# Down projection by seven block products, with weight block sums on GpSimd and the residual stream kept token-major

## The chip, the cores and the metric

One core of a Trainium2 chip runs the program. The metric is device time in microseconds (us). Engines: PE (TensorE, matrix products), DVE (VectorE) and ACT (ScalarE) for elementwise work, POOL (GpSimd) for elementwise work in SBUF, SP (SyncE), which issues the weight transfers.

## What is computed

Two encoder layers over 256 tokens of width 2048, all in float32: an RMS norm, one input projection, three kinds of attention, an output projection added to the residual stream `x`, and then a gated feed-forward block (FFN) added to `x`, which is the part that changes:

```python
def conv_ffn(x, w_up, conv_w, conv_b, w_down):       # x (256, 2048), w_up (2048, 11264), w_down (5632, 2048)
    h = x @ w_up
    hp = jnp.pad(h, ((0, 0), (1, 1), (0, 0)))
    h = hp[:, :s] * conv_w[0] + hp[:, 1:s + 1] * conv_w[1] + hp[:, 2:] * conv_w[2] + conv_b
    gate, up = jnp.split(h, 2, axis=-1)
    return (jax.nn.silu(gate) * up) @ w_down
...
        x = x + y @ w_out[l]
        x = x + conv_ffn(rms_norm(x, ffn_norm[l]), w_up[l], conv_w[l], conv_b[l], w_down[l])
    return rms_norm(x, final_norm)
```

## The kernel before

**Number format.** Every float32 product is made of three products of rounded operands (fp32r): with `a = ah + al` and `w = wh + wl`, it takes `ah*wh + al*wh + ah*wl`. So each weight chunk that lands in SBUF (tile `wland`, 128 partitions x 1024 values, 512 KB) passes ACT, which rounds it to `wh` (`emit_high`, L291), and DVE, which subtracts `wl = wland - wh` (`emit_low`, L302). Both read SBUF alone. There are 5 landing buffers and 3 to 4 buffers for the two parts (L276). 802 chunks are used in the whole run.

**Layout.** The residual stream is held transposed: `x[m]` has 128 of the 2048 features on partitions and all 256 tokens along the free axis. The activations of a product are pairs of tiles `pg` (high and low part, 256 tokens each).

**FFN.** 44 blocks `f` of 128 columns make up the 5632 hidden features. `up(g)` (L1041) computes the gate half and the up half of 11 such blocks; each block takes four chunks, and each chunk eight matmuls of 512 columns (the stationary `wh` block against high and low activations side by side) and eight of 256 (`wl` against the high ones). `conv_gen` (L1004) follows per block: ACT copies the PSUM result to `hs`, DVE adds the other half, DVE multiplies by the norm factor `rall`, ACT and DVE do the three-tap convolution (`scalar_tensor_tensor`, four per block), ACT the silu, DVE the gate product, and ACT and DVE split the result into high and low part. `down(g)` (L1084) multiplies 11 hidden blocks by `w_down`, for eight pairs of 128 output features, through `cols` (L393). Its first three groups use 512-column matmuls (`joint`), the last one 256-column matmuls. `down_gen` adds the sums to `x`. The four groups run as up(0), up(1), down(0), up(2), down(1), up(3), down(2), down(3).

**Output projection.** The same `cols`, with 256-column matmuls.

**Order.** All engines follow a static order. The PE order is the order of the code; the other steps are generators, which `pump` (L340) advances between matmuls when a small cost model (`Clock`, `Engine.cost`, L145) says that their inputs are there. POOL does only the norm's power function on a few values and the small rope tables (L1101).

Of the kernel before, what the change touches and what calls it, by code (L numbers as in the profile page):

```python
# [33 lines left out]
FGRP = 4  # L35
FPG = NF // FGRP

# [21 lines left out]
def plan():  # L59
# [7 lines left out]
    def down(g):  # L67
        for m in range(KD // 2):
            cols("w_down", list(range(g * FPG, (g + 1) * FPG)), m * 256, 256)

    def up(g):
        for f in range(g * FPG, (g + 1) * FPG):
            for half in range(2):
                for base in (0, DFF):
                    out.append(("w_up", list(range(half * 8, half * 8 + 8)), base + f * P, P))
# [12 lines left out]
    for ks in (Y_BA, Y_C):  # L88
        for m in range(KD // 2):
            cols("w_out", ks, m * 256, 256)  # L90
    up(0)
    for g in range(1, FGRP):
        up(g)
        down(g - 1)
    down(FGRP - 1)
    return out


PLAN = plan()
# [4 lines left out]
for _name, _w in (("attn_norm", 16), ("ffn_norm", 16), ("out_norm", 16), ("c_q_norm", 4), ("c_kv_norm", 4),  # L104
                  ("conv_w0", 88), ("conv_w1", 88), ("conv_w2", 88), ("conv_b", 88), ("final_norm", 16)):
    VEC[_name] = _n
    _n += _w
# [31 lines left out]
class Engine:  # L139
# [5 lines left out]
    def cost(self, op, aps, out):  # L145
        n = out.free_size()
        if self.name == "pe":
            return n * (1 if aps[1].dtype == F32R else 4) / 2.4
        if self.name == "act":
            return (112 + n) / 1.2 + 93 * sum(a.free_size() == 1 for a in aps[1:])  # L150
        return (66 + n) / 0.96 if self.name == "dve" else 500 + n / 0.6
# [36 lines left out]

class Fixed:
# [14 lines left out]
class Norm:  # L204


    def __init__(self, parts, width, squares):
        self.parts, self.left, self.width, self.squares = parts, parts, width, squares
        self.rows, self.all = [], []


class Group(Norm):


    def __init__(self, heads, k0, act, gain, squares):
        super().__init__(heads, heads * HD, squares)
# [4 lines left out]
class Kern:  # L221
    def __init__(self, tc, ctx, a):
# [7 lines left out]
        self.n_dma = self.n_high = self.n_low = self.n_use = 0  # L230
        self.land, self.high, self.parts, self.ready, self.ends = {}, {}, {}, {}, []
        self.chunks = []
        off = {m: 0 for m in MATS}
        for layer in range(DEPTH):
            for mat, ks, c0, w in PLAN:
                sz = len(ks) * w
                self.chunks.append((mat, off[mat], len(ks), w))
                off[mat] += sz * P
# [4 lines left out]
        self.pg = Slots(self.clock, self.sb, 39, "pg", [P, 2, S])  # L243
        self.pp = Slots(self.clock, self.sb, 6, "pp", [P, 2, S])
        self.tm = Slots(self.clock, self.sb, 3, "tm", [P, NB, 512])
        self.scr = Slots(self.clock, self.sb, 2, "scr", [P, NB, 512])
# [31 lines left out]
    def emit_dma(self):  # L278
        i = self.n_dma
        if i < len(self.x):  # L280
            self.load(self.nc.sync, self.x[i], self.a["x"][i].rearrange("p (j s) -> p j s", j=2))
        mat, off, nk, w = self.chunks[i]
        sz = nk * w
        t = self.t("wland", [P, CHUNK], self.LAND)
        c = self.clock
        c.at["dma"] = max(c.at["dma"], c.at["dve"])
        self.load(self.nc.sync, t[:, :sz], self.a[mat][off:off + P * sz].rearrange("(p f) -> p f", p=P))
        self.land[i] = t
        self.n_dma += 1

    def emit_high(self):  # L291
        i = self.n_high
        _, _, nk, w = self.chunks[i]
# [4 lines left out]
        self.ac.copy(h[:, :sz], self.land[i][:, :sz])  # L298
# [3 lines left out]
    def emit_low(self):  # L302
        i = self.n_low
        _, _, nk, w = self.chunks[i]
# [5 lines left out]
        self.ve.tensor_tensor(lo[:, :sz], self.land.pop(i)[:, :sz], h[:, :sz].bitcast(F32), ALU.subtract)  # L310
# [4 lines left out]
    def prefetch(self):  # L315
# [4 lines left out]
        while self.n_dma < min(n, self.LAND):  # L320
            self.emit_dma()
        while self.n_high < min(n, u + ahead + (u > 0)):
            if self.n_high >= self.n_dma:
                self.emit_dma()
# [5 lines left out]
        while self.n_dma < min(n, self.n_low + self.LAND):  # L330
            self.emit_dma()
# [61 lines left out]
    def cols(self, pm, act, ks, free, joint=False):  # L393

        mmul = self.te.matmul
        for run in k_runs(ks, 256):
            wh, wl = self.use()
            for i in range(2):
                cs = slice(i * P, (i + 1) * P)
                o = pm[:, i, :S]  # L400
                for j, k in enumerate(run):
                    self.drain(lambda: k in act)
                    x, first = act[k], k == ks[0]
                    if joint:
                        mmul(pm[:, i], wh[:, j, cs], x.rearrange("p s n -> p (s n)"), start=first, stop=False)
                    else:
                        mmul(o, wh[:, j, cs], x[:, 0], start=first, stop=False)
                        mmul(o, wh[:, j, cs], x[:, 1], start=False, stop=False)
# [42 lines left out]
    def new_norm(self):  # L451
        return Norm(KD // 2, D, self.t("sqx", [P, S], 2))
# [6 lines left out]
    def x_parts(self, m, act, gain):  # L459

        x = self.x[m]
        yield from self.until(x)
        sl = yield from self.take(self.pg, 2, F32R)
        for i in range(2):
            self.ac.activation(sl[i][:, 0], x[:, i], AF.Copy, scale=gain[:, 2 * m + i:2 * m + i + 1])
        for i in range(2):
            h, lo = self.hl(sl[i])
            self.ve.scalar_tensor_tensor(lo, x[:, i], gain[:, 2 * m + i:2 * m + i + 1], h.bitcast(F32),
                                         ALU.mult, ALU.subtract)
            act[2 * m + i] = sl[i]  # L470
        yield

    def add_squares(self, norm, x):

        yield from self.until(x)
# [788 lines left out]
```

## Time and profile before

| | us |
|---|---|
| median of 3 runs | 2286.79 (2286.78 to 2286.97) |
| profiled execution, its own time | 2286.59 |
| span of the profile, first to last instruction | 2284.8 |
| PE busy | 2263.7 (99%) |
| DVE busy | 1644.1 (72%) |
| ACT busy | 1217.7 (53%) |
| POOL busy | 32.9 (1%) |

The span is cut by stage as follows: the FFN of layer 0 runs from 398.9 to 1140.3 us on PE and that of layer 1 from 1529.5 to 2270.9 us. TensorE's granted clock is 1.00 in both stretches, which is the 2.4 GHz level. The rest is attention, the projections around it, a start of about 6 us and a tail of about 14 us. A busy time is the union of an engine's instruction spans; spans of consecutive instructions overlap a little, so the distance from start to start is what an instruction costs in a full queue.

### The profile page before, as it was taken

What the parts mean: (1) busy time and instruction counts of PE and PEld (TensorE: products, weight loads), DVE (VectorE), ACT (ScalarE), POOL (GpSimd) and SP (SyncE); (2) the same over time, 40 slices, a digit from 0 to 9 for tenths busy, and PEclk for the clock granted to TensorE, in tenths of its full rate; (3) what the DMA queues carried; (4) which work ended last, traced back from release to release, by engine and by line L of the source; (5) the groups of instructions that cost most, each with busy time, mean ns of one, the idle gap of its engine ahead of it and who ended that gap; (6) DMA issues with size and microseconds to landing.
All of it is one profiled execution on the core that took longest, in us unless ns stands there. A gap on an engine that the chain in (4) does not pass through costs nothing. (4 is left out here: it accounts for less than half of the span.)

```text
span 2284.8 us, 34786 instructions
## 1 busy us (share of the span) xinstructions
PE 2263.7 (99%) x13452; PEld 2009.3 (88%) x13452; DVE 1644.1 (72%) x2369; ACT 1217.7 (53%) x1778; POOL 32.9 (1%) x51
## 2 busy tenths in 40 slices
PE   8999999999999999999999999999999999999997
PEld 7889889888888888888988898898888888888897
DVE  6577778777766776776756877787777677667755
ACT  6456745555544554553545566555555455445543
POOL 1000000000000000000010000000000000000000
PEclk9999999999999999999999999999999999999999
DMA  7544435555555555555554444465555555555553
GB/s 275 183 147 149 161 116 189 193 185 191 186 180 198 187 186 190 191 181 186 191 188 173 157 148 140 136 198 185 188 190 184 185 194 191 181 194 191 182 186 121
DMA packets 119110, 410.15 MB, mean 180 GB/s; under 512 B 13344, under 2 KB 13856, under 8 KB 118944
## 3 DMA queue, kind: packets, MB, share of 16 engines
q1 hardware_dynamic: 118800, 407.90, 52.4%
q8 instruction: 105, 1.72, 0.3%
q14 instruction: 61, 0.50, 0.1%
q10 hardware_dynamic: 144, 0.03, 0.0%
HBM read 405.78 MB, written 2.10 MB: 179 GB/s over the span
## 5 line engine op out<-in xcount | busy, mean ns | idle before, releaser
L164 DVE TENSOR_TENSOR wl<-wland,wh 128x1024 fp32r<-128x1024 f32 (+2 forms) x802 | 943.6, 1177 | 497.3 <-PE mm L164 448.0
L164 PE MATMUL mm<-pg,wh 128*128 128x512 f32 (+1 forms) x5472 | 1274.1, 368 | 0.4 <-DVE pg L164 0.4
L164 ACT CAST wh<-wland 128x1024 fp32r<-128x1024 f32 (+2 forms) x802 | 810.7, 1011 | 761.3 <-PE mm L164 399.7
L164 PEld LDWEIGHTS mm<-pg,wh 128*128 128x128 f32 x5472 | 905.6, 190 | 120.0 <-PE mm L164 0.7
L164 PEld LDWEIGHTS mm<-pg,wl 128*128 128x128 f32 x4832 | 690.2, 190 | 60.3
L164 PE MATMUL mm<-pg,wl 128*128 128x256 f32 x4832 | 724.4, 282 | 0.0
L164 PE MATMUL mm<-wh,pg 128*128 128x512 f32 (+3 forms) x1504 | 435.9, 366 | 6.4 <-ACT pg L164 6.4
L164 PEld LDWEIGHTS mm<-wh,pg 128*128 128x128 f32 x1504 | 272.7, 189 | 46.6 <-ACT pg L164 6.4
L164 PE MATMUL mm<-wl,pg 128*128 128x512 f32 (+3 forms) x752 | 272.6, 362 | 0.3 <-DVE wl L164 0.2
L164 DVE SCALAR_TENSOR_TENSOR pp<-hs,vecs,pp 128x256 f32<-128x256 f32 x352 | 162.3, 482 | 6.3
L164 PEld LDWEIGHTS mm<-wl,pg 128*128 128x128 f32 x752 | 142.7, 190 | 19.8 <-DVE wl L164 1.2
L164 DVE TENSOR_TENSOR x<-x,mm 128x512 f32<-128x512 f32 x160 | 109.2, 683 | 6.9 <-PE mm L164 4.7
L164 ACT ACTIVATE pp<-hs,vecs 128x256 f32<-128x256 f32 x176 | 96.2, 594 | 15.5 <-DVE hs L164 15.5
L164 ACT CAST pg<-pp 128x256 fp32r<-128x256 f32 x88 | 35.8, 407 | 89.6 <-DVE pp L164 89.5
L164 ACT ACTIVATE pp<-pp 128x256 f32<-128x256 f32 x88 | 36.9, 419 | 86.7 <-DVE pp L164 86.7
L164 DVE TENSOR_TENSOR pg<-pp,pg 128x256 fp32r<-128x256 f32 x88 | 37.4, 425 | 38.7 <-ACT pg L164 38.7
L164 DVE TENSOR_TENSOR hs<-hs,rall 128x512 f32<-128x512 f32 x88 | 60.9, 692 | 3.1
L164 DVE TENSOR_TENSOR hs<-mm,hs 128x512 f32<-128x512 f32 x88 | 60.1, 683 | 0.0
L164 ACT COPY hs<-mm 128x512 f32<-128x512 f32 x88 | 51.1, 580 | 0.0
L164 PE MATMUL at<-pg,pg 128*128 128x256 f32 (+1 forms) x288 | 43.4, 294 | 0.0
L164 PEld LDWEIGHTS at<-pg,pg 128*128 128x128 f32 x288 | 38.3, 192 | 3.4 <-DVE pg L164 0.4
L164 POOL TENSOR_TENSOR small<-small,cst 128x2 f32<-128x2 f32 (+1 forms) x19 | 19.0, 1004 | 1480.4 <-DVE small L164 1480.4
(87 smaller groups left out, 790.8 us busy)
## 6 DMA issues: line engine op xcount, KB each, us to landing
wland<-in_w_up SPq DMA_DIRECT2D x352, 512.0 KB, 3.5
wland<-in_w_in SPq DMA_DIRECT2D x144, 512.0 KB, 3.5
wland<-in_w_down SPq DMA_DIRECT2D x128, 512.0 KB, 3.6
wland<-in_w_out SPq DMA_DIRECT2D x64, 384.0 KB, 3.0
wland<-in_w_down SPq DMA_DIRECT2D x64, 384.0 KB, 3.1
wland<-in_w_out SPq DMA_DIRECT2D x16, 512.0 KB, 3.5
wland<-in_w_ukv SPq DMA_DIRECT2D x12, 512.0 KB, 3.4
wland<-in_w_in SPq DMA_DIRECT2D x8, 480.0 KB, 3.2
```

The costliest lines, as they stand in the source:

```text
L164: return f(*args, **kw)
```

## The change

1. The down projection is done in 2x2 blocks after Strassen and Winograd, with seven products in place of eight. The hidden blocks come in 11 groups of four (`FPG = 4`). In each group the activation is split by token half (two of 128) and by feature half, and the weight by feature half and by output half (512 columns each, two column pairs `cp` cover 2048). Each product has 256 hidden features (two `j`), the stationary operand is an activation of 128 x 128, the moving one a weight block of 512 columns, and each takes 2 x 3 matmuls of 512 columns (`mm3`). Per layer that is 11 groups x 2 column pairs x 7 products = 154 products and 924 matmuls.
2. The weight side needs four sums of blocks per column pair and group: T1 to T4, each 128 x 1024 values. POOL makes them from the landed blocks (`emit_land`). The seven operands then pass ACT and DVE as chunks like any other, so a layer's down projection uses 154 chunks of 1024 values.
3. The activation side needs four sums of 128 x 128 per pair of hidden blocks, also on POOL (`conv_gen`). The split in high and low part is done for a pair at a time (512 and 384 values).
4. The multiplication by the norm factor in `conv_gen` goes from DVE to POOL.
5. The seven results are combined into `x` by `down_gen`: per seven products three `x` additions from PSUM and two partial sums on DVE, two copies on ACT, and six `x` additions on POOL (on DVE for the very last column pair of a layer).
6. The products are interleaved with the up blocks (`ffn_steps`): from the sixth up block on, three or four products follow each up block. 37 up blocks are followed by 3.5 on average, the last two by two each, and 21 products stand alone at the end of a layer.
7. The residual stream lies with tokens on partitions (`x[b][q]`, 128 tokens x 512 features). The output projection uses `rows` with 512-column matmuls; each norm needs 32 transposes of 128 x 128 on PE, 128 in the whole run, to make the activations. The sums of squares come from ACT's accumulator, so the DVE additions into `sqx` go.
8. The landing tiles, `tm` and `scr` become one pool `big` of 12 slots; the planner's costs per instruction are new numbers.

```diff
+def ffn_steps():
+    out, queue = [], []
+    for f in range(NF):
+        out.append(("up", f))
+        g, r = divmod(f - LAG, FPG)
+        if g >= 0 and r == FPG - 1:
+            queue += [("down", g, cp, p) for cp in range(2) for p in range(7)]
+        n = 2 if f >= NF - LAG else 4 - f % 2
+        out += queue[:n]
+        del queue[:n]
...
+        sub = lambda o, x, y: self.po.tensor_tensor(o, x, y, ALU.subtract)
+        if p == 0:
+            for b in BLOCKS:
+                t[b] = load(self.where[(*off, b)], CHUNK, 2 if b == "B11" else 3)
+        elif p == 3:
+            t["T1"], t["T2"] = slot(2), slot(2)
+            sub(t["T1"], t["B12"], t["B11"])
...
+            sub(t["T2"], t["B22"], t["T1"])
...
+        elif p == 4:
+            t["T3"] = t["B12"]
+            sub(t["T3"], t["B22"], t["B12"])
...
+        elif p == 6:
+            t["T4"] = t["B21"]
+            sub(t["T4"], t["T2"], t["B21"])
...
             self.ve.tensor_tensor(hm, pm[:, :, :S], hm, ALU.add)
             self.mm.put(pm)
-            self.ve.tensor_tensor(hm, hm, norm.all[0].to_broadcast([P, 2, S]), ALU.mult)
+            yield
+            self.po.tensor_tensor(hm, hm, norm.all[0].to_broadcast([P, 2, S]), ALU.mult)
...
+            self.po.tensor_tensor(t[:, S1], a21, t[:, A22], ALU.add)
+            self.po.tensor_tensor(t[:, S3], t[:, A11], a21, ALU.subtract)
+            self.po.tensor_tensor(t[:, S2], t[:, S1], t[:, A11], ALU.subtract)
+            self.po.tensor_tensor(t[:, S4], t[:, A12], t[:, S2], ALU.subtract)
...
+        def down_gen(g, cp, p, pt):
+            late = g == FGRP - 1 and cp == 1
+            adder = self.ve if late else self.po
+            def add(o, t):
+                adder.tensor_tensor(o, o, flat(t), ALU.add)
+            if p == 0:
+                self.ac.copy(flat(s), y)
+                add(x(1, 1), s)
+            elif p == 1:
+                self.ve.tensor_tensor(x(1, 1), x(1, 1), y, ALU.add)
...
+            elif p == 3:
+                self.ve.tensor_tensor(flat(u), y, flat(st["s1"]), ALU.add)
+                add(x(1, 2), u)
+            elif p == 4:
+                self.ve.tensor_tensor(flat(u), y, flat(st["u2"]), ALU.add)
+                add(x(2, 1), u)
+                add(x(2, 2), u)
...
+        def down(g, cp, p):
+            pt = self.at.new()
+            wh, wl = self.use()
+            side, i = SIDE[p] % 4, SIDE[p] // 4
+            for j in range(2):
+                o = G[2 * g + j]
+                self.mm3(pt.rearrange("p a s -> p (a s)"), o[i][:, side], o[2 + i][:, side], wh[:, j], wl[:, j],
+                         j == 0, j == 1)
...
         for ks in (Y_BA, Y_C):
-            for m in range(KD // 2):
+            for q in range(NQ):
                 pm = self.take_mm()
-                self.cols(pm, yact, ks, m == KD // 2 - 1, ks is Y_BA)
+                self.rows(pm, yact, ks, 512, True, True, q == NQ - 1)
```

The order of POOL's instructions before, from the attention of layer 0 to the start of layer 1 (`small` is a norm's power function, `ta` and `tb` the rope tables). The whole FFN of layer 0 lies between `small_4317` and `ta_1341_11191`:

```order
L164 TENSOR_TENSOR small_2604<-small_2602,cst 128x2
L164 TENSOR_TENSOR small_3531<-small_3529,cst 128x2
L164 TENSOR_TENSOR small_4317<-small_4315,cst 128x2
L164 TENSOR_TENSOR ta_1341_11191<-cst,again_11188 128x128
L164 TENSOR_TENSOR tb_1342_11192<-cst,again_11188 128x2x32 x2
```

POOL had nothing to do there. After the change its order in the middle of that FFN reads as follows (`gp` the four activation sums of a pair, `hs` the multiplication by the norm factor, `x` the additions of results, `big` the weight sums):

```order
L196 TENSOR_TENSOR gp_7503<-gp_7503 128x128 x4
L196 TENSOR_TENSOR hs_82<-hs_82,rall_4114 128x2x256
L196 TENSOR_TENSOR x_69<-x_69,pp_7744 128x512
L196 TENSOR_TENSOR x_72<-x_72,pp_7762 128x512
L196 TENSOR_TENSOR x_73<-x_73,pp_7762 128x512
L196 TENSOR_TENSOR x_69<-x_69,pp_7775 128x512
L196 TENSOR_TENSOR x_73<-x_73,pp_7775 128x512
L196 TENSOR_TENSOR big_7887<-big_7736,big_7732 128x1024
L196 TENSOR_TENSOR big_7888<-big_7738,big_7887 128x1024
L196 TENSOR_TENSOR big_7736<-big_7738,big_7736 128x1024
L196 TENSOR_TENSOR hs_83<-hs_83,rall_4114 128x2x256
L196 TENSOR_TENSOR x_66<-x_66,pp_7908 128x512
```

With one more `big`, these are the 16 POOL instructions (counting `x4` as four) that two up blocks and seven products bring; the pattern goes on through the FFN. All of them read two operands from SBUF.

The order of DVE before, in the FFN of layer 0, for one up block (`wl` is the subtraction for a weight chunk):

```order
L164 TENSOR_TENSOR hs_96<-mm_7380,hs_96 128x2x256
L164 TENSOR_TENSOR hs_96<-hs_96,rall_4353 128x2x256
L164 TENSOR_TENSOR wl_7513<-wland_7385,wh_7486 128x1024
L164 SCALAR_TENSOR_TENSOR pp_7521<-hs_96,vecs,pp_7521 128x256 x4
L164 TENSOR_TENSOR wl_7544<-wland_7410,wh_7511 128x1024
L164 TENSOR_TENSOR pp_7540<-pp_7540,pp_7521 128x256
L164 TENSOR_TENSOR pg_7557<-pp_7540,pg_7557 128x256
L164 TENSOR_TENSOR wl_7570<-wland_7441,wh_7542 128x1024
L164 TENSOR_TENSOR wl_7593<-wland_7467,wh_7568 128x1024
```

And DVE after, from one up block on (`at` is the PSUM result of a product, `gp` the gated block):

```order
L196 TENSOR_TENSOR hs_83<-mm_5836,hs_83 128x2x256
L196 TENSOR_TENSOR wl_5967<-big_5866,wh_5949 128x1024
L196 TENSOR_TENSOR x_66<-x_66,at_5948 128x512
L196 TENSOR_TENSOR wl_5983<-big_5892,wh_5965 128x1024
L196 TENSOR_TENSOR x_67<-x_67,at_5964 128x512
L196 SCALAR_TENSOR_TENSOR pp_5976<-hs_83,vecs,pp_5976 128x256 x4
L196 TENSOR_TENSOR wl_6009<-big_5914,wh_5981 128x1024
L196 TENSOR_TENSOR wl_6033<-big_5938,wh_6007 128x1024
L196 TENSOR_TENSOR gp_5878<-pp_6029,pp_5976 128x256
L196 TENSOR_TENSOR wl_6060<-big_5786,wh_6031 128x1024
L196 TENSOR_TENSOR pg_6070<-gp_5878,pg_6068 128x512
L196 TENSOR_TENSOR pg_6071<-gp_5878,pg_6069 128x384
```

The subtractions stand closer together, additions from PSUM stand between them, and the multiplication by `rall` is gone from this engine.

## Rows read from the trace of the kernel before

**Rows 1.** The page, part 1: engine, busy us (share of the span) x instructions.

```profile
PE 2263.7 (99%) x13452; PEld 2009.3 (88%) x13452; DVE 1644.1 (72%) x2369; ACT 1217.7 (53%) x1778; POOL 32.9 (1%) x51
```

**Rows 2.** Waits: who waited for whom, us in total, times, longest us.

```profile
PE mm L164 <- ACT pg L164: 6.4, 1, 6.4
PE at L164 <- DVE sqx L164: 2.4, 1, 2.4
...
DVE wl L164 <- PE mm L164: 448.0, 527, 2.0
```

**Rows 3.** Windows of both FFNs: us, busy us by engine, PEclk, DMA share.

```profile
398.90:1140.30 741.40, 741.40 (x4412) 659.11 (x4411) 537.99 (x720) 384.29 (x520) 0.70 (x1) 1.00 0.55 188
1529.50:2270.90 741.40, 741.12 (x4409) 658.65 (x4408) 530.13 (x704) 381.50 (x516) 0.70 (x1) 1.00 0.54 184
```

**Rows 4.** Timeline of PE, an up block: start us, us, instructions.

```profile
1003.65 2.00 PE L164 MATMUL mm<-pg,wh 128*128 128x512 f32 x8
1005.49 1.12 PE L164 MATMUL mm<-pg,wl 128*128 128x256 f32 x8
1006.45 2.00 PE L164 MATMUL mm<-pg,wh 128*128 128x512 f32 x8
```

**Rows 5.** Timeline of PE, a 512-column product of two activation parts.

```profile
63.91 0.62 PE L164 MATMUL mm<-wh,pg 128*128 128x512 f32 x2
64.36 0.39 PE L164 MATMUL mm<-wl,pg 128*128 128x512 f32 x1
64.59 0.62 PE L164 MATMUL mm<-wh,pg 128*128 128x512 f32 x2
```

**Rows 6.** Timeline of PE, the last down group of layer 0.

```profile
1137.73 0.88 PE L164 MATMUL mm<-pg,wh 128*128 128x256 f32 x6
1138.45 0.52 PE L164 MATMUL mm<-pg,wl 128*128 128x256 f32 x3
1138.81 0.88 PE L164 MATMUL mm<-pg,wh 128*128 128x256 f32 x6
```

**Rows 7.** Timeline of DVE while POOL makes rope tables, start of layer 1.

```profile
1143.35 1.22 DVE L164 TENSOR_TENSOR wl<-wland,wh 128x1024 fp32r<-128x1024 f32 x1
1144.50 0.68 DVE L164 TENSOR_TENSOR sqx<-sqx,pp 128x256 f32<-128x256 f32 x1
...
1145.21 0.43 DVE L164 TENSOR_TENSOR sqx<-sqx,pp 128x256 f32<-128x256 f32 x1
1145.57 1.34 DVE L164 TENSOR_TENSOR wl<-wland,wh 128x1024 fp32r<-128x1024 f32 x1
```

**Rows 8.** Timeline of POOL in the same stretch.

```profile
1144.14 0.75 POOL L164 TENSOR_TENSOR ta<-cst,again 128x128 f32<-128x128 f32 x1 [734.54 <-DMA again<-in_a_q_norm]
...
1144.86 0.50 POOL L164 TENSOR_TENSOR tb<-cst,again 128x64 f32<-128x64 f32 x1
...
1145.32 0.50 POOL L164 TENSOR_TENSOR tb<-cst,again 128x64 f32<-128x64 f32 x1
1145.78 1.44 POOL L164 TENSOR_TENSOR ta<-cst,again 128x128 f32<-128x128 f32 x1
```

**Rows 9.** Timeline of POOL where DVE runs nothing with two SBUF operands.

```profile
1147.74 0.47 POOL L164 TENSOR_TENSOR ta<-cst,again 128x128 f32<-128x128 f32 x1
```

**Rows 10.** Groups by form, FFN of layer 0: busy us, mean ns, idle.

```profile
L164 DVE TENSOR_TENSOR wl<-wland,wh 128x1024 fp32r<-128x1024 f32 x241 | 294.8, 1223 | 143.3 <-PE mm L164 142.6 <-issue 0.6
L164 ACT CAST wh<-wland 128x1024 fp32r<-128x1024 f32 x241 | 252.1, 1046 | 210.9 <-issue 115.8 <-PE mm L164 65.4 <-DVE x L164 27.8
L164 DVE SCALAR_TENSOR_TENSOR pp<-hs,vecs,pp 128x256 f32<-128x256 f32 x176 | 81.1, 482 | 3.1
...
L164 DVE TENSOR_TENSOR x<-x,mm 128x512 f32<-128x512 f32 x56 | 38.2, 683 | 0.8
...
L164 DVE TENSOR_TENSOR pg<-pp,pg 128x256 fp32r<-128x256 f32 x44 | 18.7, 425 | 19.4 <-ACT pg L164 19.4
```

More of the change, by code (lines that the diff above doesn't have):

```diff
@@ L88, in plan, with blocks @@
     for ks in (Y_BA, Y_C):
[L89 to L95, printed above, removed]
-    return out
+        for q in range(NQ):
+            cols("w_out", ks, q * 512, 512)
+    for step in FFN:
+        if step[0] == "up":
+            up(step[1])
+        else:
+            out.append(("w_down", *step[1:]))
+    return out
+OPS = ("B11", "B21", "B22", "T2", "T3", "T1", "T4")
+A11, A12, A22, S1, S2, S3, S4 = range(7)
+SIDE = (A11, A12, S4, S2, S3, S1, A22)
+BLOCKS = ("B11", "B21", "B12", "B22")
+def blocks(g, cp):
+    k0 = g * FPG
+    return {f"B{i + 1}{j + 1}": ([k0 + i, k0 + 2 + i], cp * 1024 + j * 512) for i in range(2) for j in range(2)}
+def ffn_steps():
[8 more added lines that the diff above has]
+        del queue[:n]
+    for g in range((NF - LAG) // FPG, FGRP):
+        queue += [("down", g, cp, p) for cp in range(2) for p in range(7)]
+    return out + queue
+LAG = 2
+NQ = D // 512
+FFN = ffn_steps()
 PLAN = plan()
@@ L276, with load_x @@
     LAND, SPLIT = 5, 3
[L278 to L284, printed above, removed]
-        c = self.clock
[L286 to L289, printed above, removed]
+    def load_x(self):
+        q = self.n_x
+        for b in range(NB):
+            self.load(self.nc.sync, self.x[b][q], self.a["x"][b * P:(b + 1) * P, q * 512:(q + 1) * 512])
+        self.n_x += 1
@@ L303, in emit_low @@
         i = self.n_low
[L304 removed]
+        _, _, nk, w, _ = self.chunks[i]
         sz = nk * w
@@ L491, in rstd_rows @@
             yield
+        if isinstance(norm, Norm):
+            yield from self.until(norm.ss)
+            s = self.small(2)
+            self.ve.tensor_reduce(s, norm.ss, AX.X, ALU.add)
+            norm.rows.append(self.rstd(s, D, 2))
+            return
         yield from self.until(norm.squares)
@@ L510, in rstd_all @@
             self.te.matmul(pt[:, 0, b * P:(b + 1) * P], self.ones, dg[b], start=True, stop=True)
-        if not copied:
-            norm.all.append(pt[:, 0])
-            return
         yield
@@ L981, in attention, with out_gen @@
         fact, fnorm = {}, self.new_norm()
-        def out_gen(m, pm, last):
-            for part in range(1 if last else 2):
-                self.ve.tensor_tensor(self.x[m], self.x[m], pm[:, :, part * S:(part + 1) * S], ALU.add)
+        def out_gen(q, pm, last):
+            for b in range(NB):
+                self.ve.tensor_tensor(self.x[b][q], self.x[b][q], pm[:, b], ALU.add)
             self.mm.put(pm)
@@ L1084, in down @@
-        def down(g):
-            for m in range(KD // 2):
-                pm = self.take_mm()
-                self.cols(pm, gT, list(range(g * FPG, (g + 1) * FPG)), m == KD // 2 - 1, g < FGRP - 1)
-                self.urgent.append(down_gen(m, pm, g == FGRP - 1))
-        up(0)
-        for g in range(1, FGRP):
-            up(g)
-            down(g - 1)
-        down(FGRP - 1)
+            n = f // 2
+            if n not in pairs:
+                t = yield from self.take(self.gp)
+                if n in pairs:
+                    self.gp.put(t)
+                else:
+                    pairs[n] = t
@@ new lines, in conv_gen, with up @@
+            self.gp.put(t)
+            G[n] = o
+        def up(f):
+            pm = self.take_mm()
+            for half in range(2):
+                for i in range(2):
+                    wh, wl = self.use()
+                    for high in (True, False):
+                        for j in range(8):
+                            k = half * 8 + j
+                            self.drain(lambda: k in act)
+                            x = act[k]
+                            if high:
+                                self.te.matmul(pm[:, i], wh[:, j], x.rearrange("p s n -> p (s n)"),
+                                               start=k == 0, stop=False)
+                            else:
+                                self.te.matmul(pm[:, i, :S], wl[:, j], x[:, 0], start=False, stop=k == KD - 1)
+                                if f == NF - 1 and i == 1:
+                                    self.pg.put(act.pop(k))
+                            if j == 7 or (high and j == 3):
+                                self.pump()
+            self.urgent.append(conv_gen(f, pm))
@@ L1095, in ffn @@
+        for step in FFN:
+            if step[0] == "up":
+                up(step[1])
+            else:
+                down(*step[1:])
         return nact, nnorm
```

382 lines of the change are left out of this document (235 added, 147 removed).

## The prediction

> **What bounds the kernel now.** I read the page first: PE is busy 99% of the span, DVE 72%, ACT 53%, POOL 1% [rows 1]. The waits come second, since a busy PE may still be a PE that is fed late: PE's two longest waits are 6.4 us once, at the start, and 2.4 us once, at the end, while DVE waits 448.0 us for PE to free `wl` buffers [rows 2]. So PE sets the time, DVE has slack, and the time of a stage is its matmuls times their distance. Third, the windows of the two FFNs: 741.4 us each with PE busy throughout, DVE 538 and 530 us, POOL 0.7 us, granted clock 1.00 [rows 3]. The distances from start to start are 1.84/8 = 0.230 us for the 512-column matmuls of an up block, 0.96/8 = 0.120 us for 256 columns there [rows 4], 0.68/3 = 0.227 us in a product of 512 columns throughout [rows 5], and 1.08/9 = 0.120 us in the last down group [rows 6]. Check: 352 up chunks at 8 x 0.350 = 2.80 us are 986 us; the first three down groups are 1056 steps of 0.350 us and the last 352 steps of 0.360 us, together 496 us. The sum, 1482 us, is the two windows' 1482.8.
>
> **The change on PE.** The down projection becomes 2 x 924 = 1848 matmuls of 512 columns at 0.227 us, 419 us for 496: minus 77 us. The output projection had 512 steps of three 256-column matmuls (184 us) and gets 768 matmuls of 512 columns (174 us): minus 10 us. The 128 new transposes of `x` are bounded by zero and by the distance of a 256-column matmul, 15 us; I take 15, since nothing stands beside them on PE. The diagonal and `sqx` work that goes from the ends of the norms lies in a microsecond or two. If PE stays the bound, the profiled execution's 2286.6 us (0.2 below the median of the runs shown, 2286.79) becomes 2286.6 - 77 - 10 + 15 = 2215.
>
> **What DVE, ACT and POOL then have to do.** Take two up blocks and seven products, the pattern of the new order. PE needs 8 x 2.80 + 42 x 0.227 = 31.9 us, 16.0 per up block. DVE has 15 `wl` subtractions at 1.22 us, eight `scalar_tensor_tensor` at 0.48, seven additions of 512 values with an operand in PSUM at 0.68 and four smaller ones of about 0.42 to 0.68 [rows 10]; that is 18.3 + 3.8 + 4.8 + 2.1 = 29.0 us, 14.5 per up block. ACT has 15 casts of 1.05 us [rows 10] and some 6 us besides, 11 per up block. Alone, both fit beside PE.
>
> POOL is the new load, and its instructions must be read together with DVE's. The only place of the trace where POOL does elementwise work beside a busy DVE is the making of the rope tables. The `wl` subtraction of DVE ends at 1143.35 + 1.22 = 1144.57; POOL's `ta`, started at 1144.14, ends at 1144.89, 0.32 later [rows 7, 8], though the same instruction takes 0.47 us when left alone [rows 9]. The second `ta` starts at 1145.78, under a `wl` subtraction that ends at 1146.91, and ends at 1147.22: 1.44 us, again 0.31 after DVE. In between they take turns: `sqx` ends at 1145.18, `tb` at 1145.36, `sqx` at 1145.64, `tb` at 1145.82. DVE is held as well: the first `sqx` takes 0.68 us for the usual 0.42, the second `wl` 1.34 for 1.22. No instruction of the one runs through an instruction of the other; each of these has two operands in SBUF. I read this as one door for both engines, held for a whole instruction.
>
> From these ends the price of a turn follows. POOL: 0.32 us for 128 values and 0.18 for 64, so 2.2 ns per value and 0.04 fixed: 0.32, 1.17 and 2.29 us for 128, 512 and 1024 values. The trace has no POOL instruction of more than 128 values, so the last two are estimates. DVE behind POOL: 0.29 us for 256 values and 1.09 for 1024, and by the line between them 0.55 for 512 and 0.42 for 384.
>
> The Trainium skill ("SBUF — State Buffer", section "Who interferes with whom") says that the second read and write path of DVE is the one of GpSimd, that it is locked for a whole instruction, and that a DVE instruction with two SBUF inputs competes for it while one with a single SBUF input does not. The turns in rows 7 and 8 agree with the lock; no row shows a long GpSimd instruction under it, or the free passage of one-input instructions. By the page the floor below would hold, and the additions from PSUM would hide beside POOL; without that second half the sum goes to the upper end below.
>
> **The sum by the door.** Per two up blocks and seven products:
> - DVE with two SBUF operands: 15 x 1.09 + 10 x 0.285 + 0.55 + 0.42 = 20.2 us.
> - POOL: four weight sums of 2.29, six additions to `x` and two norm multiplications of 1.17, four activation sums of 0.32: 9.2 + 9.4 + 1.3 = 19.8 us.
>
> Together 40.0 us, 20.0 per up block, where PE needs 16.0. So in the interleaved stretch, 37 up blocks per layer, the door is the bound: 740 us. The first five up blocks have no products and stay with PE, 5 x 11.2 = 56 us. The last two, with four products, need 16.9 + 12.9 = 30 us. The 21 products at the end need 21 x 1.09 + 12 x 2.29 + 12 x 1.17 + 6 x 0.55 = 68 us, where PE would need 28. That makes 894 us per layer and 1788 for both, where PE needs 986 + 419 = 1405. The FFNs cost 383 us more than in the PE sum: 2215 + 383 = 2598 us. This is the lower end.
>
> The upper end: DVE also has 88 + 132 + 88 = 308 instructions with one operand in PSUM. If none of them runs beside POOL (an in-order DVE may stand before one, waiting for PE, while POOL has nothing either), they add 308 x 0.68 = 210 us [rows 10]: 2808 us. Nothing in the trace says how many find POOL working; I take the middle, **2700 us**. What now waits is PE, for `wl` and for a free PSUM buffer: behind POOL's norm multiplication stand the rest of `conv_gen` and with it the next up block's buffer, behind its weight sums ACT's cast and DVE's subtraction of that chunk, and DVE, which works in order, holds everything else behind that subtraction.
>
> The weight transfers keep their bytes (176 chunks of 512 KB for 128 and 64 smaller ones) and their queue had room, a share of 0.55 in the FFN [rows 3]; I cost them at nothing, and a slower PE leaves them more room.
>
> **Rivals.**
> - *PE stays the bound, faster.* Either the turns seen are an accident of small instructions, or POOL runs in the gaps of DVE. Then DVE's 14.5 and ACT's 11 of 16.0 us hide, only the 21 products at the end are DVE's (7 x 1.22 + 5 x 0.7 = 12 us per set for 9.5, 16 us in all), and the time is 2215 to 2235 us. For it: DVE's 28% idle time [rows 1]. Against it: every overlap of two-operand instructions in rows 7 and 8 shows a wait that ends just as the other is through.
> - *A long POOL instruction gives the door up in between.* If it needs it for a share r of its time, an up block takes 10.1 + 9.9 r us. Up to r = 0.6 PE hides it (2215 to 2240 us); at r = 0.70 the kernel is as slow as before; at 0.85 it takes about 2400 us. For it: rows 8 have only 64 and 128 values. Against it: there the time grows by 2.2 ns with each value and DVE is let in only at the end.
> - *Worse than all turns.* The weight sums are a chain: the second waits for the first, ACT's cast for it, DVE's subtraction for that. If DVE stands still for one 2.29 us sum in each of the 44 sets of seven products while nothing else can use the time, 100 us come on top of the upper end: 2908 us. Against it: five chunks are landed ahead, some 13 us of work at the new pace.
>
> **Chances.** The door with its two ends, 2598 to 2808 us: 0.66. Worse than that: 0.12. Partial hold: 0.10, with 0.04 of it faster than before. PE stays the bound: 0.12. So faster 0.16, within 0.2% 0.01, slower 0.83 (0.2%, 4.6 us, is about what a measurement of this kernel can tell from no change). The range: the low end goes to 2400 us, to take in a hold of more than 0.85 of an instruction; the high end goes to 2880, most of the way to the worst case. The likeliest case's own range is 2598 to 2808.
>
> **What would show it.** In the profile after, PE's busy share should fall from 99% to about 80 to 85%, with PE waiting for DVE's `wl`. POOL's 1024-value sums should show far more than 2.3 us each, DVE's `wl` subtractions more than 1.22, and neither should overlap the other by more than about 0.2 us of work; DVE's additions from PSUM should keep 0.68 us. In the windows the interleaved stretch should take about 20 to 22 us per up block. The prediction is wrong if the `wl` mean stays at 1.22 us beside POOL sums of 2.3 us; then the door is not shared for long instructions, and the time is near 2215 us. The PE terms are right if a product's six matmuls stand 0.227 us apart wherever PE is not waiting.

## The result and the profile after

The changed kernel takes 2732.24 us (median of 4 runs, 2730.61 to 2732.45) where the kernel before takes 2286.88 (4 runs, 2286.78 to 2287.36): a ratio of 1.1945, 95% interval 1.1925 to 1.1966. The forecast was 2700 with a range of 2400 to 2880. The profiled execution took 2732.21 us, with a span of 2730.4 and a mean granted clock of 0.934.

The page's first part, busy time of each engine, answers to [rows 1]:

```profile
PE 2344.2 (86%) x11788; PEld 1971.8 (72%) x11788; DVE 2326.9 (85%) x2408; ACT 1377.7 (50%) x1990; POOL 1278.5 (47%) x744
```

PE has lost its 99%. DVE's share went from 72% to 85% and POOL's from 1% to 47%. The waits answer to [rows 2] (columns: us in total, times, the longest):

```profile
PE mm L196 <- DVE wl L196: 173.3, 39, 5.5
PE at L196 <- DVE wl L196: 124.9, 94, 2.8
PE at L196 <- ACT pg L196: 23.0, 4, 11.3
PE at L196 <- DVE pp L196: 18.6, 12, 7.3
...
DVE wl L196 <- PE mm L196: 152.2, 121, 2.6
```

Before, DVE stood 448 us waiting for PE to free `wl`. Now PE stands 298 us waiting for DVE to fill it. The windows of the two FFNs answer to [rows 3], and under them two pieces of the steady stretch, each 43.0 us long (columns as in [rows 3]). The pattern of two up blocks and seven products comes back every 42.5 us there, so each piece holds it once and a little more:

```profile
414.00:1361.40 947.40, 778.85 (x3761) 647.20 (x3759) 884.00 (x757) 461.10 (x606) 623.24 (x348) 0.91 0.44 146
1768.60:2716.50 947.90, 779.27 (x3753) 646.87 (x3751) 884.21 (x759) 460.40 (x611) 621.74 (x347) 0.91 0.42 141
...
700.00:743.00 43.00, 37.23 (x173) 30.93 (x172) 40.96 (x35) 20.63 (x27) 28.93 (x16) 0.88 0.45 147
743.00:786.00 43.00, 34.97 (x173) 29.29 (x173) 40.96 (x36) 20.58 (x27) 28.89 (x16) 0.92 0.43 148
```

The FFNs went from 1482.8 to 1895.3 us, which is 412.5 of the 445.6 us by which the span grew. An up block, with its three or four products, takes 21.3 us. In 43.0 us DVE is busy for 40.96, POOL for 28.9; an instruction that is held at its start by the other engine counts as busy. What this busy time consists of is read from the groups by form, which answer to [rows 10] (after the bar: busy us, mean ns of one, idle time before):

```profile
L196 DVE TENSOR_TENSOR wl<-big,wh 128x1024 fp32r<-128x1024 f32 x886 | 1294.4, 1479 | 187.1 <-PE mm L196 140.3 <-issue 28.3 <-ACT wh L196 12.7
L196 POOL TENSOR_TENSOR big<-big,big 128x1024 f32<-128x1024 f32 x176 | 510.4, 2910 | 28.1 <-issue 24.7
L196 POOL TENSOR_TENSOR x<-x,pp 128x512 f32<-128x512 f32 x252 | 465.7, 1873 | 5.0 <-ACT pp L196 4.7
L196 DVE SCALAR_TENSOR_TENSOR pp<-hs,vecs,pp 128x256 f32<-128x256 f32 x352 | 425.6, 1228 | 6.2
L196 DVE TENSOR_TENSOR gp<-pp,pp 128x256 f32<-128x256 f32 x88 | 121.9, 1385 | 0.5 <-ACT pp L196 0.5
L196 DVE TENSOR_TENSOR x<-x,at 128x512 f32<-128x512 f32 x132 | 89.1, 675 | 0.0
```

Three kinds of DVE instruction with two operands in SBUF became longer: `wl` from 1223 to 1479 ns, `scalar_tensor_tensor` from 482 to 1228, the `gp` product to 1385. POOL's 1024-value sums take 2910. The additions that read PSUM (`x<-x,at`) take 675 ns, as [rows 10] have it for their kind. A mean of 1479 hides two populations; the timelines of DVE and of POOL in one stretch show them (start us, duration us):

```profile
703.58 1.21 DVE L196 TENSOR_TENSOR wl<-big,wh 128x1024 fp32r<-128x1024 f32 x1
704.71 0.67 DVE L196 TENSOR_TENSOR x<-x,at 128x512 f32<-128x512 f32 x1
705.31 1.61 DVE L196 TENSOR_TENSOR wl<-big,wh 128x1024 fp32r<-128x1024 f32 x1
706.84 0.68 DVE L196 TENSOR_TENSOR x<-x,at 128x512 f32<-128x512 f32 x1
707.44 4.37 DVE L196 SCALAR_TENSOR_TENSOR pp<-hs,vecs,pp 128x256 f32<-128x256 f32 x4
711.73 1.22 DVE L196 TENSOR_TENSOR wl<-big,wh 128x1024 fp32r<-128x1024 f32 x1
```

```profile
703.73 2.11 POOL L196 TENSOR_TENSOR hs<-hs,rall 128x512 f32<-128x512 f32 x1 [5.50 <-DVE hs L196]
705.80 2.27 POOL L196 TENSOR_TENSOR x<-x,pp 128x512 f32<-128x512 f32 x1
708.03 2.58 POOL L196 TENSOR_TENSOR big<-big,big 128x1024 f32<-128x1024 f32 x1
```

The second `wl` starts at 705.31 under POOL's `hs`, which ends at 705.84, and takes 1.61. POOL's `x` starts at 705.80, under that `wl`, which ends at 706.92; POOL ends at 708.07, 1.15 later. The PSUM additions at 704.71 and 706.84 run their 0.67 and 0.68 us through POOL's turns. The four `scalar_tensor_tensor`, 1.9 us by [rows 10], take 4.37 since POOL's `big` comes among them. The last `wl` starts after POOL's `big` has ended at 710.61 and takes the old 1.22. These are the turns of [rows 7, 8], with longer instructions.

### The profile page after: what moved, and what is told of

Read it like the earlier page. It is cut to its first block, busy times and chain, and to the rows that moved or that the text cites. A ratio compares the mean times of both kernels' runs of the same rounds, so it can differ in the third digit from the quotient of the medians.

```text
span 2730.4 us, 33196 instructions
## 1 busy us (share of the span) xinstructions
PE 2344.2 (86%) x11788; PEld 1971.8 (72%) x11788; DVE 2326.9 (85%) x2408; ACT 1377.7 (50%) x1990; POOL 1278.5 (47%) x744
## 4 chain that ended last, share of the span: by engine, by line
PE 58%; DVE 26%; issue 8%; POOL 5%; ACT 2%; DVEq 0%; DMA 0%; SPq 0%; POOLq 0%; ACTq 0%
PE mm L196 47%; DVE wl L196 14%; PE at L196 11%; DVE pp L196 9%; POOL gp L196 4%; ACT pg L196 1%; POOL x L196 1%; DVE pg L196 1%; DVE hs L196 1%; ACT pp L196 0%; DVE gp L196 0%; DVE x L196 0%; DVEq L196 0%; POOL big L196 0%; DVE small L196 0%
## 5 line engine op out<-in xcount | busy, mean ns | idle before, releaser
L196 DVE TENSOR_TENSOR wl<-big,wh 128x1024 fp32r<-128x1024 f32 x902 | 1310.8, 1471 | 201.1 <-PE mm L196 152.2
L196 ACT CAST wh<-big 128x1024 fp32r<-128x1024 f32 x902 | 925.7, 1043 | 760.7 <-PE mm L196 401.5
L196 PE MATMUL mm<-pg,wh 128*128 128x512 f32 (+1 forms) x3008 | 776.2, 402 | 1.2 <-DVE pg L196 1.2
L196 PEld LDWEIGHTS mm<-pg,wh 128*128 128x128 f32 x3008 | 571.2, 201 | 108.2 <-DVE pg L196 2.0
L196 PE MATMUL mm<-pg,wl 128*128 128x256 f32 x2912 | 446.7, 299 | 172.5 <-DVE wl L196 172.5
L196 PEld LDWEIGHTS mm<-pg,wl 128*128 128x128 f32 x2912 | 426.6, 206 | 214.9 <-DVE wl L196 189.4
L196 POOL TENSOR_TENSOR big<-big,big 128x1024 f32<-128x1024 f32 x176 | 510.4, 2910 | 28.1 <-issue 24.7
L196 POOL TENSOR_TENSOR x<-x,pp 128x512 f32<-128x512 f32 x252 | 465.7, 1873 | 5.0 <-ACT pp L196 4.7
L196 PE MATMUL at<-wh,pg 128*128 128x512 f32 x1232 | 420.3, 413 | 37.1 <-ACT pg L196 22.6
L196 DVE SCALAR_TENSOR_TENSOR pp<-hs,vecs,pp 128x256 f32<-128x256 f32 x352 | 425.6, 1228 | 6.2
L196 PE MATMUL at<-wl,pg 128*128 128x512 f32 x616 | 266.3, 432 | 125.4 <-DVE wl L196 124.9
L196 POOL TENSOR_TENSOR hs<-hs,rall 128x512 f32<-128x512 f32 x88 | 141.9, 1612 | 420.8 <-DVE hs L196 420.8
```

The lines of the kernel that those rows point to most:

```text
L196: return f(*args, **kw)
```

## The experiments

The theory: DVE and POOL share one door to SBUF, held for a whole instruction by any instruction with two SBUF operands on DVE or any on POOL that reads SBUF; where products follow the up blocks, the FFN's length is little more than the sum of both engines' turns. The rivals: DVE is late for another reason (its own load, its place in the order, a chain over a slow POOL), or PE's granted clock of 0.91 is a cause. The runs e1 to e6 are one execution each; the four of the changed kernel lie within 2 us.

**e1_bench**, a program of its own: streams of eight instructions (24 in one case), alone and side by side; `acc` lies in PSUM, all else in SBUF. The four loops, cut to their instructions:

```python
            def pool(n, k):
...
                    nc.gpsimd.tensor_tensor(po[i % 4][:, :n], bar[:, :n], src[0][:, :n], ALU.subtract)
...
                    nc.gpsimd.memset(po[i % 4][:, :n], 0.5)
...
                    nc.vector.tensor_tensor(ve[i % 4][:, :n], bar[:, :n], src[1][:, :n], ALU.subtract)
...
                    nc.vector.tensor_tensor(ve[i % 4][:, :n], bar[:, :n], acc[:, :n], ALU.subtract)
```

> A kernel of its own, not the encoder: stages one after the other, eight GpSimd subtractions of 1024 or 512 values and eight VectorE subtractions, first alone, then side by side; GpSimd also beside VectorE subtractions with one operand in PSUM, and GpSimd memsets beside VectorE. Shared door, held for a whole instruction: alone 2.3 us for 1024 values on GpSimd and 1.15 on VectorE; side by side the eight pairs take turns, 8 x (2.3 + 1.1) = 27 us, no shorter than the sum; with one operand in PSUM the stage is as long as the longer engine alone, about 18 to 19 us, and memsets do not stretch VectorE. A door that a long instruction gives up in between: side by side well under 27 us, near 19 us. No shared door: 19 us side by side.

It ran 140.31 us. Its timeline, DVE's and POOL's rows (start, duration of the eight or 24 together); first the streams alone, then side by side, and at the end three single instructions from the middle of the pairs:

```profile
9.77 18.45 POOL L40 TENSOR_TENSOR po<-bar,src 128x1024 f32<-128x1024 f32 x8 [9.33 <-ACT po L36]
39.95 9.17 DVE L48 TENSOR_TENSOR ve<-bar,src 128x1024 f32<-128x1024 f32 x8 [39.95 <-ACT bar L56]
49.86 4.87 DVE L52 TENSOR_TENSOR ve<-bar,acc 128x512 f32<-128x512 f32 x8 [0.74 <-ACT bar L55]
...
61.28 24.18 DVE L48 TENSOR_TENSOR ve<-bar,src 128x1024 f32<-128x1024 f32 x8 [6.55 <-ACT bar L56]
61.39 26.27 POOL L40 TENSOR_TENSOR po<-bar,src 128x1024 f32<-128x1024 f32 x8 [1.31 <-ACT bar L56]
...
100.37 14.44 DVE L52 TENSOR_TENSOR ve<-bar,acc 128x512 f32<-128x512 f32 x24 [1.80 <-ACT bar L55]
101.00 18.51 POOL L40 TENSOR_TENSOR po<-bar,src 128x1024 f32<-128x1024 f32 x8 [1.31 <-ACT bar L56]
...
119.42 7.23 POOL L44 MEMSET po<- 128x1024 f32 x8
120.71 9.17 DVE L48 TENSOR_TENSOR ve<-bar,src 128x1024 f32<-128x1024 f32 x8 [5.90 <-ACT bar L56]
...
64.67 3.32 POOL L40 TENSOR_TENSOR po<-bar,src 128x1024 f32<-128x1024 f32 x1
65.71 3.36 DVE L48 TENSOR_TENSOR ve<-bar,src 128x1024 f32<-128x1024 f32 x1
67.95 3.32 POOL L40 TENSOR_TENSOR po<-bar,src 128x1024 f32<-128x1024 f32 x1
```

Alone, POOL takes 18.45/8 = 2.30 us (1.22 for 512 values) and DVE 9.17/8 = 1.15. Side by side both streams need 26.27/8 = 3.28 us for a pair: they add, less 0.17 us per pair. By the ends of the single instructions, POOL's at 67.99, DVE's at 69.07 and POOL's at 71.27, DVE's turn takes 1.08 us and POOL's 2.20. With an operand in PSUM nothing is added to either stream (14.44/24 = 0.60 beside POOL, 4.87/8 = 0.61 alone; POOL 18.51). Nor does a memset on POOL slow DVE (9.17 both times). The forecast had 1.09 for DVE's turn and 2.29 for POOL's, the second extended from instructions of 64 and 128 values. For the last two pairs the Trainium skill ("SBUF — State Buffer", section "Who interferes with whom") says that a DVE instruction with two SBUF inputs contends with a GpSimd instruction that reads SBUF, not with one that only writes it, and that one with at most one SBUF input, outside DVE's two-port modes, doesn't contend. This trace agrees with both, by the 9.17 and the 18.51 us.

**e2_none**: all FFN work of POOL is left out (weight sums, activation sums, norm multiplications, additions by POOL to `x`), so that its output isn't the reference's.

```diff
-            sub(t["T1"], t["B12"], t["B11"])
...
+            t["T1"], t["T2"], t["T3"], t["T4"] = t["B11"], t["B22"], t["B12"], t["B21"]
...
-            self.po.tensor_tensor(hm, hm, norm.all[0].to_broadcast([P, 2, S]), ALU.mult)
...
-            self.po.tensor_tensor(t[:, S1], a21, t[:, A22], ALU.add)
...
-                adder.tensor_tensor(o, o, flat(t), ALU.add)
+                pass
```

> All GpSimd work of the feed-forward blocks is left out (weight sums, activation sums, norm multiplication and additions to x), everything else is kept, so the output is not the reference's. Shared door, and also a theory that GpSimd is merely a slow queue which others wait for: TensorE is the bound, 2215 to 2235 us, granted clock back near 1.0. If VectorE's own new load (14.5 us of 16.0 per up block) is the cause: over 2400 us.

Measured: 2255.18 us, beside 2287.44 for the kernel before. The windows of its two FFNs:

```profile
413.70:1132.80 719.10, 711.21 (x3775) 611.69 (x3775) 601.60 (x765) 471.57 (x621) 6.62 (x13) 1.00 0.60 193
1529.90:2242.70 712.80, 706.71 (x3753) 607.76 (x3751) 597.34 (x756) 466.86 (x616) 0.70 (x1) 1.00 0.58 187
```

They take 1431.9 us, where the PE sum was 1405; `wl` is back at 1223 ns and `scalar_tensor_tensor` at 482. It misses the expected 2215 to 2235 by 20 us, for two reasons: the end of an FFN, where the 21 products that follow each other take 46 and 40 us in place of PE's 28, and about 19 us more outside the FFNs than before, where the sum has 5. So PE's saving is real and 477 us come with POOL's work.

**e3_all_dve** and **e4_sums_dve**: all of POOL's FFN work on DVE, and the weight sums alone on DVE. The first change is in both, the others are in e3 alone.

```diff
-        sub = lambda o, x, y: self.po.tensor_tensor(o, x, y, ALU.subtract)
+        sub = lambda o, x, y: self.ve.tensor_tensor(o, x, y, ALU.subtract)
...
-            self.po.tensor_tensor(hm, hm, norm.all[0].to_broadcast([P, 2, S]), ALU.mult)
+            self.ve.tensor_tensor(hm, hm, norm.all[0].to_broadcast([P, 2, S]), ALU.mult)
...
-            self.po.tensor_tensor(t[:, S1], a21, t[:, A22], ALU.add)
...
+            self.ve.tensor_tensor(t[:, S1], a21, t[:, A22], ALU.add)
...
-            adder = self.ve if late else self.po
+            adder = self.ve
```

> All GpSimd work of the feed-forward blocks is done by VectorE instead, nothing is left out. Shared door: per two up blocks VectorE then has 20.2 + 4.8 us of its own and 9.5 us for what took GpSimd 19.8 us at the door, 34.5 us against TensorE's 31.9, so 2360 to 2440 us: one engine alone is faster than two. If VectorE's own load is the cause, the added work makes it slower than 2732 us. If the two engines do work at the same time, VectorE becomes the bound with more work than either has now: about 2730 us or more.

> Only the weight sums go from GpSimd to VectorE. Shared door: per two up blocks the door has 24.6 us of VectorE and 10.6 of GpSimd, 35.2 at the least and 40.0 if no one-input instruction hides; with the same half hidden as in the changed kernel 18.8 us per up block, about 2460 us. If the chain of weight sums on GpSimd (second sum behind the first, cast behind it) is what holds TensorE, most of the loss goes: near 2300 us.

Measured: 2524.82 and 2567.89 us. Both came out above what was expected. The window of 43 us in e3, which now holds more than two up blocks:

```profile
700.00:743.00 43.00, 39.77 (x202) 33.02 (x201) 42.54 (x61) 24.68 (x32) 0.00 (x0) 0.96 0.48 156
```

DVE is busy for 42.54 of 43 us: with all on one engine, an up block takes 18.7 us in the mean of the 37 that have products, where 17.25 were expected. The expectation priced DVE's instructions as turns behind POOL, `wl` at 1.09 us and 256 values at 0.285; with nothing on POOL they cost 1.14 and 0.44 from start to start. In e4 the steady part was near the expected, 19.2 us per up block for 18.8. The rest of both misses lies at the ends of the FFNs, where the last 21 products take 69 to 77 us, and outside the FFNs, some 26 us more than before. The rival of e4, that the chain of weight sums on a slow POOL is the cause and that 2300 us come back once it is short, falls. What counts is the order of the times: 2525 with one engine, 2568 with POOL doing a part, 2732 with POOL doing all. One engine is 207 us faster than two.

**e5_memset**: POOL's elementwise instructions become memsets of about their length (its output isn't the reference's). The order of DVE, ACT and PE stays the same, instruction by instruction.

```diff
+def fill(eng, o, *ins):
...
+    for x in (o, o, o[:, :1] if len(o.shape) > 2 else o[:, :o.shape[1] // 2]):
+        eng.engine.memset(x, 0.5)
-        sub = lambda o, x, y: self.po.tensor_tensor(o, x, y, ALU.subtract)
+        sub = lambda o, x, y: fill(self.po, o, x, y)
...
-            self.po.tensor_tensor(hm, hm, norm.all[0].to_broadcast([P, 2, S]), ALU.mult)
+            fill(self.po, hm, norm.all[0])
...
+            for i in (S1, S3, S2, S4):
+                fill(self.po, t[:, i])
...
+                    fill(self.po, o, t)
```

> Each GpSimd subtraction, addition and multiplication of the feed-forward blocks becomes memsets of the same tile that take about the same time (two and a half times the tile, 0.95 us per 1024 values), so GpSimd writes but reads nothing, and the output is not the reference's; the order of VectorE is word for word that of the changed kernel. Shared door for reads: TensorE is the bound again, 2255 us as without GpSimd work, up to 2290 with the waits for it. If GpSimd is a slow queue that the others wait for, whatever it does: 2600 to 2732 us.

Measured: 2282.94 us. Page part 1 and the `wl` group:

```profile
PE 2198.5 (96%) x11788; PEld 1894.0 (83%) x11788; DVE 1756.0 (77%) x2408; ACT 1387.9 (61%) x1990; POOL 995.5 (44%) x2128
...
L196 DVE TENSOR_TENSOR wl<-big,wh 128x1024 fp32r<-128x1024 f32 x886 | 1080.1, 1223 | 375.0 <-PE mm L196 237.6 <-issue 117.9 <-ACT wh L196 13.0
```

POOL is busy for 44% of the span and still stands between DVE and ACT at `hs` (it waits 367.8 us for DVE there, and ACT 63.9 us for it), and 449 of the 477 us are gone. With its reads go POOL's waits for what it read; the longest of them in the changed kernel, 420.8 us at `hs`, stays, since the memset writes the same tile. So it isn't that POOL takes long, or that others wait for it, that makes the time, but that its instructions read SBUF beside DVE's.

**e6_warm**: ten matmuls of 256 columns, whose result is overwritten, ahead of each product.

```diff
+            k = self.kr[0]
+            for _ in range(10):
+                self.te.engine.matmul(pt.rearrange("p a s -> p (a s)")[:, :S], k[:, :P], k, start=True, stop=True)
```

> Ten extra matmuls of 256 columns on constant data ahead of each of the 308 products, to keep TensorE busy while it waits; the other engines' order is unchanged. The extra 4.2 us per up block fit in the 5.3 that TensorE waits. Shared door alone: 2725 to 2790 us, no gain, with the granted clock near 1.0. If the half clock, granted for 363 us of the changed kernel, is a cause of the loss: down by a good part of 180 us, below 2650.

Measured: 2762.47 us, 30 more than the changed kernel, with a granted clock of 0.990. The window of the first FFN:

```profile
414.00:1377.00 963.00, 910.42 (x5298) 792.06 (x5296) 880.51 (x761) 475.63 (x605) 626.26 (x355) 0.99 0.45 145
```

With the clock at 0.99 in place of 0.91 the FFN is no shorter, and DVE's 880 busy us are the 884 of before. The filler has a price of its own, PE busy for 910 us in place of 779, so a small gain from the clock could hide in it; the good part of 180 us that this rival needs isn't there. The lower clock goes with PE's waits and doesn't make the loss.

**e7_eight**: the residual stream with tokens on partitions, but the down projection with eight products.

```diff
-            queue += [("down", g, cp, p) for cp in range(2) for p in range(7)]
+            queue += [("down", g, q) for q in range(NQ)]
```

> The token-major residual stream and the 512-column products are kept, but the down projection has eight products again (plain 512-column matmuls, results added from PSUM on VectorE, nothing on GpSimd). TensorE's terms: 17 us less in the down projection than before, 10 less in the output projection, 15 more for the transposes and some 19 more outside the feed-forward blocks, as in the run without GpSimd work: 2294 us, 2280 to 2305. If the layout itself costs more than that: over 2310.

Measured: 2295.38 us in the median of five executions, ratio 1.0039 (1.0025 to 1.0053). The windows of its FFNs:

```profile
412.50:1149.90 737.40, 736.19 (x3910) 634.55 (x3909) 536.04 (x724) 387.70 (x518) 5.64 (x13) 1.00 0.58 189
1548.60:2282.20 733.60, 732.97 (x3885) 631.91 (x3883) 529.88 (x711) 379.99 (x503) 0.70 (x1) 1.00 0.55 182
```

The other half of the change costs some 9 us by itself. The FFNs take 1471.0 us, 12 less than before (by the sum 17 less, 2112 x 0.227 = 479 for 496), and what lies outside them takes 822.6 of the span's 2293.6, 21 more.

**e8_mixed**, **e9_spread**, **e10_spread4**: seven products for some groups of four up blocks, eight for the others, all on DVE. In e8 the groups' products stand one group after the other, up to four products of a group of seven to an up block; in e9 and e10 at most two of them go to an up block, and blocks with eight products stand between them, so that DVE's extra load is spread. Seven products have the groups 1, 3, 5, 7, 9 in e8, 0, 2, 4, 6, 8 in e9 and 1, 3, 5, 7 in e10. The lines are those of e9:

```diff
-            queue += [("down", g, cp, p) for cp in range(2) for p in range(7)]
...
+            (q7 if g in SEVEN else q8).extend(group_steps(g))
+        left = min(left + 24, 36)
+        for _ in range(2):
+            if q7:
+                out.append(q7.pop(0))
+                left -= 6
+        if q8 and left >= 24:
+            out.append(q8.pop(0))
+            left -= 24
...
+SEVEN = (0, 2, 4, 6, 8)
```

> Five of the eleven groups (1, 3, 5, 7, 9) with seven products, the other six with eight, all sums on VectorE, nothing on GpSimd. Averaged over a group, VectorE has about 59 us of work and TensorE 65, so TensorE should be the bound, with 2.7 us less per group of seven: 2294 - 27 = 2267 us, 2255 to 2285. If VectorE has no such reserve from block to block: 2290 to 2350 us.

> As the run with five groups of seven products, but groups 0, 2, 4, 6, 8 have seven, and at most two of their products follow an up block, with eight-product blocks of the other groups between them, so that VectorE's load is even. If VectorE had no reserve only within a group of seven (18.1 us per up block against TensorE's 16.0): TensorE is the bound throughout, 2295 - 27 = 2268 us, 2262 to 2282. If VectorE's load as such is too much: 2300 to 2340 us.

> The same with groups 1, 3, 5 and 7 only, which leaves no product of the seven for the end of a layer: 2295 - 22 = 2273 us, 2267 to 2285. If what stands at the end decides, this is faster than the one with five groups; if TensorE's columns decide, 5 us slower.

Measured: e8 2339.69 us, ratio 1.0233 (1.0217 to 1.0248); e9 2269.37 us, ratio 0.9923 (0.991 to 0.9937), beside 2286.72 for the kernel before; e10 2273.68, ratio 0.9943 (0.9931 to 0.9956). A window of e8 in a group of seven, and page part 1 of e9:

```profile
700.00:743.00 43.00, 39.55 (x200) 32.22 (x199) 42.82 (x56) 26.15 (x34) 0.00 (x0) 1.00 0.59 195
...
PE 2222.4 (98%) x11932; PEld 1916.9 (85%) x11932; DVE 1867.8 (82%) x2668; ACT 1293.6 (57%) x1870; POOL 32.6 (1%) x52
```

e8 missed its 2267. In the window DVE is busy for 42.82 of 43 us and PE for 39.55: beside a group of seven DVE is late, and the mean DVE load of a layer says nothing of that. A group of four up blocks with seven products takes 68 us and one with eight 66, where PE's columns alone would give 64 and 66. About half of what e8 loses to e7 lies there, the rest at the ends of the FFNs. Spread, five groups of seven keep PE at 98%, and the kernel is faster than e7 and e8. They are other five groups than in e8, but e10, with four of those of e8, gains as well. e9 is 26 us faster than e7, and leaves out 12 matmuls in each of ten groups, 120 x 0.227 = 27 us: all of what it saves on PE arrives. e10 is 4 us slower than e9 and has 24 matmuls more, 5 us: the columns decide, and not what stands at the end. Over the kernel before 17 us are left to e9, since the token-major stream costs its 9.

## Why the prediction was right

- **PE's terms** held. In a product, three matmuls stand 0.69 us apart, 0.23 each, as put:

```profile
700.04 0.62 PE L196 MATMUL at<-wh,pg 128*128 128x512 f32 x2
700.50 0.40 PE L196 MATMUL at<-wl,pg 128*128 128x512 f32 x1
700.73 0.62 PE L196 MATMUL at<-wh,pg 128*128 128x512 f32 x2
...
719.91 0.50 PE L196 MATMUL at<-wl,pg 128*128 128x512 f32 x1 [1.95 <-DVE wl L196]
```

  The 1.95 us in the last row is the new wait. With POOL's work out of the way the kernel does come to 2255 (e2). Of the two waits that the prediction names, the one for `wl` is there, with 298 us; for a free PSUM buffer there are at most the 18.6 us behind DVE's `pp`.
- **The door** is as read from rows 7 and 8: whole instructions, in turns, also for 1024 values (e1). e5 takes away what POOL reads, keeps about its time and the others' order, and the time falls to 2283. Of the rivals, "PE stays the bound" and "a long POOL instruction gives the door up in between" end with e1: a pair takes 3.28 us where the sum of both is 3.45, so that r is at least (3.28 - 1.15)/2.30 = 0.93. "Worse than all turns" is refuted by the time: 1895 us in the FFNs, under the upper end's 1998.
- **The size** was right, 1895.3 us in the FFNs for the middle's 1893 (1788 + 105), in part by luck. The rows of both engines tell what made it, if a held instruction counts from the end of the one that held it. In a steady 42.5 us, taken instruction by instruction from 716.56 us on, the turns take 40.7 us: DVE's 21.1 and POOL's 19.6, where the forecast has 40.0, 20.2 and 19.8. Behind POOL, DVE's prices are as put (`wl` 1.08 us, 256 values 0.28), but ten of the 15 `wl` don't stand behind a POOL instruction and cost 1.14; POOL's estimates were a little high (2.23 us for 2.29, 1.15 for 1.17). Five of the seven PSUM additions run while POOL is at work, for 2.9 of their 4.7 us, like the two in the timelines above; the other two find POOL with nothing to do. So 1.8 us are left beside the turns, 1.2 of them PSUM additions alone. The forecast had half of 4.8 for that, and said that no row told how many would hide: that half of them was close is the luck.
- **Where DVE's time went**, from the means of after and of e2: 886 x (1479 - 1223) = 227 us in `wl`, 352 x (1228 - 482) = 263 in `scalar_tensor_tensor`, 88 x (1385 - 420) = 85 in `gp`. The sum, 575, is more than the 477 that were lost, since part of it lay in DVE's former idle time, which fell from 505 us in e2 (2253.0 - 1747.9) to 404 (2730.4 - 2326.9).
- **The mis-sized term** lies outside the FFNs: +5 us by the sum (15 for the transposes, -10 for the output projection), and 835.1 - 802.0 = +33 measured; with the FFNs' 2 of difference and the rounding to 2700 it makes the 32 us by which the result is over the forecast. The windows ahead of the first FFN and between the two, before and after:

```profile
0.00:398.90 398.90, 391.21 (x2315) 345.88 (x2316) 290.60 (x483) 231.25 (x383) 15.82 (x28) 1.00 0.51 175
1140.30:1529.50 389.20, 388.18 (x2314) 344.21 (x2314) 278.53 (x454) 219.07 (x359) 14.96 (x20) 1.00 0.48 162
...
0.00:414.00 414.00, 394.90 (x2143) 340.08 (x2143) 274.00 (x437) 228.79 (x386) 17.05 (x29) 1.00 0.53 177
1361.40:1768.60 407.20, 391.17 (x2134) 337.69 (x2135) 276.84 (x443) 225.37 (x383) 15.80 (x20) 0.99 0.48 156
```

  PE's work is as put: 786.1 us for 779.4, and 1.8 less in the tail, is +5. The other 28 us are PE's idle time: 19.1 us for 7.7 ahead of the first FFN, 16.0 for 1.0 between the two, and 1.8 more in the tail of 13.9 us. The sum put the waits around the transposes at nothing, though `x` must now be transposed before a layer can begin. At the start, and where the second layer begins, PE shows waits that it did not have before:

```profile
4.96 0.47 PE L196 MATMUL at<-cst,x 128*128 128x128 f32 x1 [4.96 <-DMA cst<-in_cst]
10.17 0.80 PE L196 MATMUL mm<-wh,pg 128*128 128x512 f32 x1 [2.36 <-ACT pg L196]
...
1364.74 0.50 PE L196 MATMUL mm<-wh,pg 128*128 128x512 f32 x1 [3.49 <-ACT pg L196]
1367.49 1.22 PE L196 MATMUL mm<-wh,pg 128*128 128x512 f32 x2 [2.02 <-DVE pg L196]
```

  The first projection starts at 10.17 us for 6.37 before, and 5.5 us are waited between the layers: 9.3 us. Without POOL's work 19 (e2) or 21 us (e7) of the 33 remain, which is the price of the token-major stream. The other 12 to 14 us come with POOL's instructions even where these read nothing: in e5 834.8 us lie outside the FFNs. Which waits carry them no run tells.
- **PE's busy share**, 86%, is a point over the 80 to 85 forecast.

## What to carry to other kernels

Elementwise work with operands in SBUF that is moved from DVE to POOL didn't run beside DVE's own two-operand work in this case: it took DVE's door, and for twice as long as DVE would have needed (2.30 us for 1.15). So add both streams before moving any, and set POOL's work beside DVE instructions that have an operand in PSUM, which it didn't hold up in e1. And when fewer matmuls are bought with elementwise work, compare the engines stretch by stretch: five groups of seven products lost 2.3% where DVE's extra load came in a lump and gained 0.8% where it was spread.

## What the runs showed of the hardware

A PE that waits several times in each 43 us, for 1 to 5 us each, was granted a clock of 0.88 to 0.92 in those stretches, the 1.2 GHz level for 363 us in all; restoring it to 0.99 with extra matmuls gave no time back (e6), with DVE as busy as before. And a pair of DVE and POOL instructions in turns costs 0.17 us less than the two alone (3.28 for 3.45 us): the turns take a little less than the instructions' own distances.
